# Storing the rows of a seven-product matrix multiply without chained adding transfers, with raw rows, raw weights and gate weights sharing one pool

## The chip, the cores and the metric

The kernel runs on one core of a Trainium2 chip. The metric is the device time of one execution in microseconds (us), the median of the runs. The engines are PE (TensorE, matmul), PEld (its weight loads), DVE (VectorE), ACT (ScalarE), POOL (GpSimd) and SP (SyncE, which here only issues DMAs). POOL issues DMAs too, all those that add to what lies at the destination among them.

## The reference, cut to what matters

One layer of an encoder runs over 1024 prompt tokens and 32 sample tokens, which the kernel treats as T = 1056 columns. After two attention branches it ends in three parts:

```python
# ConvFFN
a, g = split(h @ w_up)                     # 1024 -> 2 x 2816
gc = conv_b + sum(conv_w[i] * gx[:, i:i+T] for i in range(3))
f = (gelu(gc) * a) @ w_down                # 2816 -> 1024
x = x + rms_norm(f, g_post_ffn)
# per-layer embedding
gate = sigmoid(rms_norm(x, g_pre_ple) @ w_ple_gate)
x = x + rms_norm(gate * (pe @ w_ple), g_post_ple)
```

Everything is float32. A matmul operand is split into a high part (rounded to float32r) and a low part (the remainder), and each product takes three matmuls: high by high, high by low, low by high.

## The kernel before

**Layout.** Activations lie with features on the 128 partitions and tokens along the row. `HT` = 528 is half of the tokens, `HC` = 264 a quarter; `one` and `two` are the two halves.

**Up product (L1103 to L1316).** The 22 feature tiles `f` of the gated FFN are made one by one, tiles 0 to 3 plainly and tiles 4 to 21 by a seven-product scheme (`up_strassen`, seven `mul` of 24 matmuls of 264 columns each). Per tile `gx` and `av` (three buffers each) take the two halves of `h @ w_up`, and `activate_steps` (L1058) makes the convolution in `gc` (one buffer), its gelu, and the product with `av`. Signs are put in, so that the seven-product scheme of the *down* product finds its operands in the DRAM tile `d_b[7, 11, 128, 528]`: seven sums of the four quarters of the 2816 x 1056 operand (top tiles f < 11 and bottom tiles f >= 11, halves `one` and `two`). Each tile writes its rows into the slots that contain it, from POOL. A top tile stores `one` to slots 0 to 3 (one transfer with a repeated source), `two` to slot 4, and then adds `two` to slots 1 to 3. A bottom tile stores to slots 5 and 6, adds `two` to slots 2 to 4, and then adds `one` to slot 3. The last transfer of either has to wait for the one before it, since both write the same rows.

From L1311 to L1316 (tiles 2 to 20 and the quarter sums) the order on the engines is set by the framework's planner; before and after, PE, DVE and ACT run in an order written out in the program (`manual_schedule`), while the planner still orders SP and POOL.

**Down product (L1322 to L1700).** 28 units `u`, seven operands `p` by four output row groups `m`. A unit is 11 blocks of 128 by 3 matmuls by 2 column halves, 66 matmuls of 264 columns, in three parts `q` (4, 4 and 3 blocks). `row_load` fetches the rows of `d_b` (tile `uraw`, three buffers), `row_split` makes their high and low parts (`d0` to `d8`); `w_load` fetches the raw weights (`wraw`, two buffers, one unit each), `w_split` makes `whi` and `wlo`. All loads go by SP, one after the other. `uraw`, `wraw` and `d0` to `d5` lie in the pool `up`, which is released after unit 27.

Between the parts stand side jobs. `gate_ahead` (L1363) loads a tile of the last part's weights `w_ple_gate` (`raw`, two buffers), splits it (`t`, three buffers) and stores the parts to `d_gate` from POOL: 8 tiles of two parts each. It comes after every part with q = 0 or 2 from unit 1 on (L1654), two parts in a unit. `last_rows_up` finishes tile 21 in unit 0. `norm_first` makes the first half's RMS norms in units 20 to 27 (`NORM_1`).

**Gate phase (L1701 to L1843).** 32 products of 24 matmuls of 264 columns: 16 for set c = 0 (8 output tiles n by two quarters), 8 for c = 1 and 8 for c = 2. The gate weights return from `d_gate` through POOL (`gate_weights`, L1604): tiles 0 and 1 into `whi` and `wlo` in unit 27, the others, 1024 KB each, into `gw` in the space that `up` leaves. Beside the products, `norm_second` makes the norms of the second half; `NORM_2` says how many of its 34 steps follow each product. Its steps 1, 12 and 28 are totals of squares (`total`), its steps 2, 15 and 29 the matmuls on those totals and the inverse roots (`own_sums`, `inverse`); step 20 completes the operand of c = 1 and step 34 that of c = 2. `LAST` places the same for the final norm: `last_total`, `last_sum`, `last_inverse` and `last_rows` (which multiplies, and adds to the output by a POOL transfer). After the last product the tail makes the final norm of c = 2 and stores it.

Of the kernel before, what the change touches and what calls it, by code (L numbers as in the profile page):

```python
# [17 lines left out]
P = 128  # L18
# [88 lines left out]
          (6, 0, 0): 1, (6, 0, 1): 1, (6, 1, 0): 1, (6, 1, 1): 1, (6, 1, 2): 1, (6, 2, 0): 1, (6, 2, 1): 1, (6, 2, 2): 1}  # L107
NORM_2 = (1, 1, 1, 2, 2, 2, 2, 2, 1, 1, 2, 2, 2, 2, 2, 2, 1, 1, 2, 2, 1)
SQUARES_2 = ((6, 0, 2), (6, 1, 0))
# [3 lines left out]
def emit(tc, a):  # L113
# [944 lines left out]
    def activate_steps(f, gx, av):  # L1058
        gc = tl(fp, [P, GW - 2], tag="gc", bufs=1)
        L = GW - 2  # L1060
        cw = [col(CONV_W + 3 * f + i) for i in range(3)]
        ac.activation(gc, gx[:, 0:L], AF.Identity, scale=cw[0], bias=col(CONV_B + f))
        yield
        ve.scalar_tensor_tensor(gc, gx[:, 1 : L + 1], cw[1], gc, op0=ALU.mult, op1=ALU.add)
        ve.scalar_tensor_tensor(gc, gx[:, 2 : L + 2], cw[2], gc, op0=ALU.mult, op1=ALU.add)
        po.tensor_copy(convo[:, f, 0:2], gx[:, NP : NP + 2])
        po.tensor_copy(convo[:, f, 2:4], gx[:, GW - 2 : GW])
        yield
        ac.activation(gc, gc, AF.Gelu_apprx_tanh)
        yield  # L1070
        top = f < HD
        for o, g, neg in ((slice(0, HT), slice(0, HT), not top), (slice(HT, NP), slice(HT, NP), top), (slice(NP, T), slice(NP + 2, None), top)):
            if neg:
                ve.scalar_tensor_tensor(av[:, o], gc[:, g], -1.0, av[:, o], op0=ALU.mult, op1=ALU.mult)
            else:
                ve.tensor_tensor(av[:, o], gc[:, g], av[:, o], op=ALU.mult)
        k = f % HD

        def to(x, i, j, **kw):
            x = x.unsqueeze(1).to_broadcast([P, j - i, HT]) if j > i + 1 else x.unsqueeze(1)  # L1080
            po.dma_start(d_b[i:j, k].rearrange("q p t -> p q t"), x, **kw)

        if top:
            to(av[:, one], 0, 4)
            to(av[:, two], 4, 5)
            to(av[:, two], 1, 4, accum_op=ALU.add)
        else:
            po.dma_start(d_b[5:7, k].rearrange("q p t -> p q t"), av.rearrange("p (q t) -> p q t", q=2))
            to(av[:, two], 2, 5, accum_op=ALU.add)
            to(av[:, one], 3, 4, accum_op=ALU.add)  # L1090

# [232 lines left out]
    WSRC = (quarter_of(0, 0), d_ws[1], d_ws[2], quarter_of(1, 1), quarter_of(0, 1), d_ws[0], d_ws[3])  # L1324
    NU = 4 * len(RSRC)
    up = pool("up", side="right")
    ub = pool("ub", side="right")
# [11 lines left out]
    def row_load(p, i):  # L1339
        if p < len(RSRC):  # L1340
            n = 2 if i < 5 else 1
            raws[p, i] = tl(up, [P, 2, HT], tag="uraw", bufs=3)[:, :n]
            dma.dma_start(raws[p, i], d_b[RSRC[p], 2 * i : 2 * i + n].rearrange("k p t -> p k t"))
# [19 lines left out]
    def gate_ahead(n):  # L1363
        raw = []

        def load():
            raw.append(tl(wp, [P, KT, P], tag="raw", bufs=2))
            dma.dma_start(raw[0], a["w_ple_gate"][n])

        def part(b):  # L1370
            c = slice(KT // 2 * b, KT // 2 * (b + 1))
            t = tl(tp, [P, 2, HT], F32R, tag="t", bufs=3)[:, :, : KT // 2 * P]
            split_rows(t[:, 0], t[:, 1], raw[0][:, c].rearrange("p k c -> p (k c)"), False)
            po.dma_start(d_gate[n].rearrange("p (x b c) -> p x b c", x=2, b=2)[:, :, b], t)

        return [load] + [lambda b=b: part(b) for b in range(2)]
# [3 lines left out]
    def w_load(u):  # L1380
        if u < NU:
            t = tl(up, [P, HD * P], tag="wraw", bufs=2)
            dma.dma_start(t, WSRC[u // 4][u % 4])
            wraw[u] = t.rearrange("p (k c) -> p k c", c=P)
# [202 lines left out]
    row_load(0, 2)  # L1587
    w_load(1)
    for q in range(3):
# [14 lines left out]
    def gate_weights(n):  # L1604
# [8 lines left out]
        else:  # L1613
            t = tl(gw, [P, 2, KT, P], F32R, tag="gw", bufs=KT - 2)
            po.dma_start(t, src)
            for b in range(0, KT, KT // 2):
                for x in range(2):
                    out[x].append(t[:, x, b : b + KT // 2])
        wgate[n] = out
# [5 lines left out]
    for load, *fs in items:  # L1625
        loads.append((len(ahead) - 4, load))
        ahead += fs
    done = 0
    norm = None
    for u in range(NU):  # L1630
# [3 lines left out]
        for q in range(3):  # L1634
            h, l = wsp.pop((u, q))
            for k in range(KS[q], KS[q + 1]):
                wh, wl = h[:, k - KS[q]], l[:, k - KS[q]]
                xh_, xl_ = [t[:, k % 2] for t in rows[p, k // 2]]
                for j in range(2):
# [3 lines left out]
                    pe.matmul(o, wl, xh_[:, s], start=False, stop=(k == HD - 1 and p in (3, 4, 6)), skip_group_check=True)  # L1643
            if q == 0:
                w_load(u + 2)
            w_split(u + 1, q)
# [4 lines left out]
            if (m, q) == (0, 0):  # L1651
                row_split(p, 5)
                row_load(p + 1, 1)
            if (u, q) > (1, 0) and q != 1 and done < len(ahead):  # L1654
                while loads and loads[0][0] <= done:
# [19 lines left out]
            if u == NU - 1 and q:  # L1675
                gate_weights(q - 1)
            for i in range(NORM_1.get((p, m, q), 0)):
                next(norm, None)
# [27 lines left out]
    norm = norm_second()  # L1706
    gate_weights(2)

# [46 lines left out]
    def gated(n, t, g):  # L1755
        zz = z[:, n, SETS[2]]
        ve.tensor_tensor(zz, t, g, op=ALU.mult)
        if n < KT - 2:
            sq = ag[2] if n == 0 else tl(gw, [P, HC], tag="sq1", bufs=2)
            ac.activation(sq, zz, AF.Square)  # L1760
        else:
            sq = tl(gw, [P, HC], tag="sq1", bufs=2)
            ve.tensor_tensor(sq, zz, zz, op=ALU.mult)
# [5 lines left out]
    def gated_sum():  # L1769
        if len(ends) == 1 and gathered[0] < KT - 3:  # L1770
# [6 lines left out]

    LAST = {(1, 3): [(last_total, 0)], (1, 5): [(last_sum, 0), (last_inverse, 0)], (1, 6): [(last_rows, 0, 0), (last_rows, 0, 2)], (1, 7): [(last_rows, 0, 4), (last_rows, 0, 6)],
            (2, 0): [(last_total, 1)], (2, 2): [(last_sum, 1), (last_inverse, 1)]}
    for i in range(4):  # L1780
        LAST[2, 3 + i] = [(last_rows, 1, 2 * i)]
    gathered = [0]
# [4 lines left out]
    for at, (c, n, j) in enumerate(parts):  # L1787
        s = SETS[c]
        if n == 0 and j == 0:
            ag[c] = tl(np_, [P, 2, HT], tag="acc", bufs=2)[:, 0, : s.stop - s.start]  # L1790
            if c == 2:
                assert next(norm, 0) == 0

                early = tl(gw, [P, 2, HC], tag="early", bufs=1)
                dma.dma_start(early, kpt(d_pl, KT - 2, s))
# [3 lines left out]
        if j == 0:  # L1799
            if c < 2 or n < KT - 2:  # L1800
                tg[c] = tl(gw, [P, HT], tag="plt", bufs=2)[:, : s.stop - s.start]
                dma.dma_start(tg[c], d_pl[n, :, s])
            else:
                tg[c] = early[:, n - KT + 2]
# [10 lines left out]
        after = None  # L1815
        if c == 0 and j == 0 and n + 3 < KT:
            gate_weights(n + 3)
        if at < len(NORM_2):
# [15 lines left out]
    for i in range(3):  # L1834
        if i == 2:
            after()
        pe.matmul(ps, onesM, (ag[2], *ends)[i], start=(i == 0), stop=(i == 2))
    gain(KT - 1)
    rs = tl(np_, [P, HT], tag="rs", bufs=1)[:, :HC]
    inverse(rs, [(ps, slice(0, HC))])  # L1840
# [5 lines left out]
    np_.release()  # L1846
    gw.release()
    wp.release()
    cst.release()
# [84 lines left out]
```

## Time and profile before

| what | value |
|---|---|
| time, median of 3 runs | 2004.07 us (2000.85 to 2005.7) |
| the profiled execution: its own time | 2003.85 us |
| the profiled execution: its span | 2001.9 us |
| mean granted TensorE clock | 0.988 |
| busy in the span: PE, DVE, ACT, POOL | 1938.0, 1234.7, 951.2, 422.7 us |
| up product of tiles 4 to 21 (1258 to 1631.6 us) | DMA share 0.65 in 1258 to 1620 |
| down product | 1631.6 to 1878.7 us |
| gate phase and tail | 1878.7 to 2001.9 us |

PE is counted busy while a matmul runs, at whatever clock; matmuls of 264 columns start some 0.12 us apart at full clock and some 0.22 us apart at half. The window view gives for each stretch the busy time of an engine with the number of its instructions, the granted clock, and the DMA engines' mean share.

### The profile page before, as it was taken

Reading aid. Unit: us, or ns where it says so; the run is one execution under the profiler, and the core shown is the slowest. Engines: PE = TensorE matmul, PEld = TensorE weight load, DVE = VectorE, ACT = ScalarE, POOL = GpSimd, SP = SyncE. Lnnn points to the kernel's source line nnn. Section 1 sums busy time; section 2 is a strip of 40 time slices with the busy share of each in tenths; the row PEclk is TensorE's granted clock in tenths of the full one; section 3 lists DMA queues with packets and bytes.
Section 4 is the critical chain, followed back from the end, with each engine's and each line's share of the span. In section 5 each row is a group of like instructions: output and inputs, shape, how many; then the busy total and the mean of one; then the engine's idle time right before and its main releaser. Section 6 shows DMA issues by size and latency. Waiting matters only on the chain.

```text
span 2001.9 us, 34483 instructions
## 1 busy us (share of the span) xinstructions
PE 1938.0 (97%) x13594; PEld 1895.5 (95%) x13594; DVE 1234.7 (62%) x2524; ACT 951.2 (48%) x1747; POOL 422.7 (21%) x479
## 2 busy tenths in 40 slices
PE   8999999999999999999999999999999998999996
PEld 7999999999999999998999999999999998999996
DVE  7556655466376474665644775776676754558675
ACT  6456456354473553662423454433333344545454
POOL 4423322242121131121220111212122111000102
PEclk9999999999999999998999999999999998999998
DMA  7112111266244272247733447866656579956636
GB/s 282 64 56 84 62 56 59 72 184 164 79 135 110 90 190 72 83 129 233 266 124 114 130 137 243 243 156 165 138 130 134 122 221 310 330 175 222 214 121 109
DMA packets 112382, 300.94 MB, mean 150 GB/s; under 512 B 11796, under 2 KB 34012, under 8 KB 111324
## 3 DMA queue, kind: packets, MB, share of 16 engines
q1 hardware_dynamic: 78780, 198.45, 30.3%
q0 software_dynamic: 33152, 99.94, 20.2%
q8 instruction: 106, 1.74, 0.3%
q14 instruction: 56, 0.46, 0.1%
q10 hardware_dynamic: 288, 0.36, 0.1%
HBM read 198.49 MB, written 123.28 MB: 161 GB/s over the span
## 4 chain that ended last, share of the span: by engine, by line
PE 70%; DVE 13%; DMA 6%; ACT 6%; issue 3%; SPq 0%; POOL 0%; DVEq 0%; ACTq 0%; POOLq 0%
PE mm L228 12%; PE mm L229 12%; PE mm L230 12%; PE two L1208 6%; PE two L1210 6%; PE two L1209 6%; PE two L1643 2%; PE two L1641 2%; PE two L1642 2%; PE one L508 2%; PE two L730 2%; DMA d_b<-av 2%; PE one L466 1%; DVE d L698 1%; DMA ev<-d_inv 1%
## 5 line engine op out<-in xcount | busy, mean ns | idle before, releaser
L228 PE MATMUL mm<-xh,whi 128*128 128x352 f32 x1248 | 412.1, 330 | 0.0
L230 PE MATMUL mm<-xh,wlo 128*128 128x352 f32 x1248 | 411.9, 330 | 0.0
L229 PE MATMUL mm<-xl,whi 128*128 128x352 f32 x1248 | 409.7, 328 | 0.0
L208 POOL TENSOR_TENSOR wlo<-raw,whi 128x512 fp32r<-128x512 f32 x130 | 188.0, 1452 | 678.8 <-ACT whi L207 626.3
L228 PEld LDWEIGHTS mm<-xh,whi 128*128 128x128 f32 x1248 | 235.2, 188 | 1.6 <-DVE ev L352 0.5
L229 PEld LDWEIGHTS mm<-xl,whi 128*128 128x128 f32 x1248 | 235.0, 188 | 1.7 <-issue 0.3
L230 PEld LDWEIGHTS mm<-xh,wlo 128*128 128x128 f32 x1248 | 234.6, 188 | 1.1
L1641 PE MATMUL two<-d,whi 128*128 128x264 f32 x616 | 178.1, 289 | 9.6 <-ACT whi L1391 7.5
L1643 PE MATMUL two<-d,wlo 128*128 128x264 f32 x616 | 177.9, 289 | 1.4 <-DVE wlo L1392 1.3
L1642 PE MATMUL two<-d,whi 128*128 128x264 f32 x616 | 177.9, 289 | 1.0 <-DVE d L1351 0.9
L207 ACT ACTIVATE whi<-raw 128x512 fp32r<-128x512 f32 (+1 forms) x146 | 89.5, 621 | 157.6 <-PE mm L229 95.2
L1210 PE MATMUL two<-mh,wlo 128*128 128x264 f32 x576 | 163.1, 284 | 0.0
L1209 PE MATMUL two<-ml,whi 128*128 128x264 f32 x576 | 163.0, 284 | 0.0
L1208 PE MATMUL two<-mh,whi 128*128 128x264 f32 x576 | 161.2, 284 | 0.0
L1641 PEld LDWEIGHTS two<-d,whi 128*128 128x128 f32 x616 | 118.4, 192 | 10.6 <-ACT whi L1391 8.3
L1643 PEld LDWEIGHTS two<-d,wlo 128*128 128x128 f32 x616 | 118.3, 192 | 2.6 <-DVE wlo L1392 2.6
L1642 PEld LDWEIGHTS two<-d,whi 128*128 128x128 f32 x616 | 118.4, 192 | 1.7 <-DVE d L1351 1.7
L1210 PEld LDWEIGHTS two<-mh,wlo 128*128 128x128 f32 x576 | 108.4, 188 | 0.0
L1209 PEld LDWEIGHTS two<-ml,whi 128*128 128x128 f32 x576 | 108.4, 188 | 0.0
L1208 PEld LDWEIGHTS two<-mh,whi 128*128 128x128 f32 x576 | 107.4, 188 | 0.0
L352 DVE TENSOR_TENSOR ev<-mm,rstd 128x352 f32<-128x352 f32 x120 | 61.4, 518 | 54.4 <-PE mm L230 53.9
L1198 ACT ACTIVATE whi<-ws 128x512 fp32r<-128x512 f32 x72 | 45.5, 633 | 102.1 <-PE two L1209 75.5
(503 smaller groups left out, 5184.1 us busy)
## 6 DMA issues: line engine op xcount, KB each, us to landing
raw<-in_w_in SPq DMA_DIRECT2D x52, 512.0 KB, 3.8
uraw<-d_b SPq DMA_DIRECT2D x36, 528.0 KB, 4.8
d_b<-av POOLq DMA_DIRECT2D x22, 792.0 KB, 9.2
d_ws<-in_w_down POOLq DMA_DIRECT2D x24, 704.0 KB, 11.7
raw<-in_w_up SPq DMA_DIRECT2D x27, 512.0 KB, 4.1
d_b<-av POOLq DMA_DIRECT2D x11, 1056.0 KB, 5.0
wraw<-d_ws SPq DMA_DIRECT2D x16, 704.0 KB, 7.9
sraw<-in_w_up SPq DMA_DIRECT2D x17, 512.0 KB, 4.9
```

The source lines that it names most:

```text
L207: ac.activation(hi[-1][:, d], raw[:, b], AF.Copy)
L208: eng.tensor_tensor(lo[-1][:, d], raw[:, b], hi[-1][:, d], op=ALU.subtract)
L228: pe.matmul(ps, h, xh(kt), start=(first and i == 0), stop=False)
L229: pe.matmul(ps, h, xl(kt), start=False, stop=False)
L230: pe.matmul(ps, l, xh(kt), start=False, stop=(last and i == n - 1))
L352: return lambda ps, s: ve.tensor_tensor(t[:, s], ps, rstd(s), op=ALU.mult)
L1208: pe.matmul(ps[:, j, :HC], w[0][:, k], x[0][:, k, s], start=st, stop=False, skip_group_check=True)
L1209: pe.matmul(ps[:, j, :HC], w[0][:, k], x[1][:, k, s], start=False, stop=False, skip_group_check=True)
L1210: pe.matmul(ps[:, j, :HC], w[1][:, k], x[0][:, k, s], start=False, stop=sp_, skip_group_check=True)
L1641: pe.matmul(o, wh, xh_[:, s], start=(k == 0 and p in (0, 4, 5)), stop=False, skip_group_check=True)
L1642: pe.matmul(o, wh, xl_[:, s], start=False, stop=False, skip_group_check=True)
L1643: pe.matmul(o, wl, xh_[:, s], start=False, stop=(k == HD - 1 and p in (3, 4, 6)), skip_group_check=True)
```

## The change

1. *Rows.* VectorE adds the two halves once (`sm`, written over `gc`). A top tile stores `one` and `two` to slots 0 and 4 in one transfer and `sm` to slots 1 to 3; nothing is added in DRAM. A bottom tile stores to slots 5 and 6, adds `two` to slots 2 and 4, and adds `sm` to slot 3. No transfer of a tile writes rows that another of the same tile writes.
2. *Pool.* `uraw` and `wraw` move to a pool `rp` that lives to the end. Gate weights 2 and 3 go into these buffers and are asked for in unit 27; the others (`gw`, now four buffers) are asked for two tiles earlier. The buffers `plt`, `early` and `sq1` of the gate phase move into tiles that exist already.
3. *Gate splits.* They come one in a unit, after q = 2, from unit 4 to unit 19, and each raw tile is asked for two parts later in the list than before. `w_load(1)` stands after the first part of unit 0.
4. *Steps.* `NORM_2` has a product more between total and sums at three places, and its last step stands after product 22 in place of 20. The entries of `LAST` come two products later; the last two rows of c = 1 are done in the tail.

```diff
-NORM_2 = (1, 1, 1, 2, 2, 2, 2, 2, 1, 1, 2, 2, 2, 2, 2, 2, 1, 1, 2, 2, 1)
+NORM_2 = (1, 0, 1, 2, 2, 2, 2, 2, 2, 0, 1, 2, 2, 2, 2, 2, 2, 1, 0, 1, 2, 2, 1)
...
+        both, sm = av.rearrange("p (q t) -> p q t", q=2), gc[:, :HT]
+        ve.tensor_tensor(sm, av[:, one], av[:, two], op=ALU.add)
         if top:
-            to(av[:, one], 0, 4)
-            to(av[:, two], 4, 5)
-            to(av[:, two], 1, 4, accum_op=ALU.add)
+            to(both, slice(0, 5, 4))
+            to(sm, slice(1, 4))
         else:
-            po.dma_start(d_b[5:7, k].rearrange("q p t -> p q t"), av.rearrange("p (q t) -> p q t", q=2))
-            to(av[:, two], 2, 5, accum_op=ALU.add)
-            to(av[:, one], 3, 4, accum_op=ALU.add)
+            to(both, slice(5, 7))
+            to(av[:, two], slice(2, 5, 2), accum_op=ALU.add)
+            to(sm, slice(3, 4), accum_op=ALU.add)
...
+    rp = pool("rp", side="right")
...
-            raws[p, i] = tl(up, [P, 2, HT], tag="uraw", bufs=3)[:, :n]
+            raws[p, i] = tl(rp, [P, 2, HT], tag="uraw", bufs=3)[:, :n]
...
-            t = tl(up, [P, HD * P], tag="wraw", bufs=2)
+            t = tl(rp, [P, HD * P], tag="wraw", bufs=2)
...
     row_load(0, 2)
-    w_load(1)
     for q in range(3):
...
-            t = tl(gw, [P, 2, KT, P], F32R, tag="gw", bufs=KT - 2)
-            po.dma_start(t, src)
+            if n < 4:
+                t = [tl(rp, [P, HD * P], F32R, tag="wraw", bufs=2) if n == 2 else tl(rp, [P, 2, HT], F32R, tag="uraw", bufs=3).rearrange("p k t -> p (k t)") for x in range(2)]
+                t = [v[:, : KT * P].rearrange("p (k c) -> p k c", c=P) for v in t]
+                for x in range(2):
+                    po.dma_start(t[x], src[:, x])
+            else:
+                t = tl(gw, [P, 2, KT, P], F32R, tag="gw", bufs=KT - 4)
+                po.dma_start(t, src)
+                t = [t[:, x] for x in range(2)]
...
-        loads.append((len(ahead) - 4, load))
+        loads.append((len(ahead) - 2, load))
...
             if q == 0:
+                if u == 0:
+                    w_load(1)
                 w_load(u + 2)
...
-            if (u, q) > (1, 0) and q != 1 and done < len(ahead):
+            if u >= 4 and q == 2 and done < len(ahead):
...
                 gate_weights(q - 1)
+                gate_weights(q + 1)
...
-    gate_weights(2)
+    gate_weights(4)
...
+        sq = g if n else ag[2]
...
-    LAST = {(1, 3): [(last_total, 0)], (1, 5): [(last_sum, 0), (last_inverse, 0)], (1, 6): [(last_rows, 0, 0), (last_rows, 0, 2)], (1, 7): [(last_rows, 0, 4), (last_rows, 0, 6)],
-            (2, 0): [(last_total, 1)], (2, 2): [(last_sum, 1), (last_inverse, 1)]}
-    for i in range(4):
-        LAST[2, 3 + i] = [(last_rows, 1, 2 * i)]
+    LAST = {(1, 5): [(last_total, 0)], (1, 7): [(last_sum, 0), (last_inverse, 0)], (2, 0): [(last_rows, 0, 0), (last_rows, 0, 2)], (2, 1): [(last_rows, 0, 4), (last_rows, 0, 6)],
+            (2, 2): [(last_total, 1)], (2, 4): [(last_sum, 1), (last_inverse, 1)]}
+    for i in range(3):
+        LAST[2, 5 + i] = [(last_rows, 1, 2 * i)]
+    plt, turn = tl(rp, [P, 2, HT], tag="uraw", bufs=3), 0
...
-                early = tl(gw, [P, 2, HC], tag="early", bufs=1)
+                early = tl(np_, [P, 2, HT], tag="accn", bufs=1)[:, :, :HC]
...
-                tg[c] = tl(gw, [P, HT], tag="plt", bufs=2)[:, : s.stop - s.start]
+                tg[c] = plt[:, turn % 2, : s.stop - s.start]
...
-        if c == 0 and j == 0 and n + 3 < KT:
-            gate_weights(n + 3)
+        if c == 0 and j == 0 and n + 5 < KT:
+            gate_weights(n + 5)
...
     gain(KT - 1)
+    last_rows(1, KT - 2)
```

More of the change, by code (lines that the diff above doesn't have):

```diff
@@ L1077, in activate_steps, with to @@
         k = f % HD
-        def to(x, i, j, **kw):
-            x = x.unsqueeze(1).to_broadcast([P, j - i, HT]) if j > i + 1 else x.unsqueeze(1)
-            po.dma_start(d_b[i:j, k].rearrange("q p t -> p q t"), x, **kw)
+        def to(x, q, **kw):
+            o = d_b[q, k].rearrange("q p t -> p q t")
+            po.dma_start(o, x if len(x.shape) == 3 else x.unsqueeze(1).to_broadcast([P, o.shape[1], HT]), **kw)
+        both, sm = av.rearrange("p (q t) -> p q t", q=2), gc[:, :HT]
+        ve.tensor_tensor(sm, av[:, one], av[:, two], op=ALU.add)
         if top:
-            to(av[:, one], 0, 4)
-            to(av[:, two], 4, 5)
-            to(av[:, two], 1, 4, accum_op=ALU.add)
-        else:
-            po.dma_start(d_b[5:7, k].rearrange("q p t -> p q t"), av.rearrange("p (q t) -> p q t", q=2))
-            to(av[:, two], 2, 5, accum_op=ALU.add)
-            to(av[:, one], 3, 4, accum_op=ALU.add)
+            to(both, slice(0, 5, 4))
+            to(sm, slice(1, 4))
+        else:
+            to(both, slice(5, 7))
+            to(av[:, two], slice(2, 5, 2), accum_op=ALU.add)
+            to(sm, slice(3, 4), accum_op=ALU.add)
     def plain_out(gx, av, j, s, ps):
@@ L1371, in part @@
             c = slice(KT // 2 * b, KT // 2 * (b + 1))
-            t = tl(tp, [P, 2, HT], F32R, tag="t", bufs=3)[:, :, : KT // 2 * P]
+            t = tl(tp, [P, 2, KT // 2 * P], F32R, tag="t", bufs=3)
             split_rows(t[:, 0], t[:, 1], raw[0][:, c].rearrange("p k c -> p (k c)"), False)
@@ L1613, in gate_weights @@
         else:
-            t = tl(gw, [P, 2, KT, P], F32R, tag="gw", bufs=KT - 2)
-            po.dma_start(t, src)
+            if n < 4:
[7 more added lines that the diff above has]
+                t = [t[:, x] for x in range(2)]
             for b in range(0, KT, KT // 2):
                 for x in range(2):
-                    out[x].append(t[:, x, b : b + KT // 2])
+                    out[x].append(t[x][:, b : b + KT // 2])
         wgate[n] = out
@@ L1757, in gated @@
         ve.tensor_tensor(zz, t, g, op=ALU.mult)
+        sq = g if n else ag[2]
         if n < KT - 2:
-            sq = ag[2] if n == 0 else tl(gw, [P, HC], tag="sq1", bufs=2)
             ac.activation(sq, zz, AF.Square)
         else:
-            sq = tl(gw, [P, HC], tag="sq1", bufs=2)
             ve.tensor_tensor(sq, zz, zz, op=ALU.mult)
@@ L1800, in emit @@
             if c < 2 or n < KT - 2:
-                tg[c] = tl(gw, [P, HT], tag="plt", bufs=2)[:, : s.stop - s.start]
+                tg[c] = plt[:, turn % 2, : s.stop - s.start]
+                turn += 1
                 dma.dma_start(tg[c], d_pl[n, :, s])
@@ L1847, in emit @@
     gw.release()
+    rp.release()
     wp.release()
```

## The prediction

> **What bounds the kernel now.** I read the page first, then PE's waits from the up product to the end, then a window table of PE over that stretch, then time lines around the losses. Page:
>
> ```profile
> span 2001.9 us, 34483 instructions
> PE 1938.0 (97%) x13594; PEld 1895.5 (95%) x13594; DVE 1234.7 (62%) x2524; ACT 951.2 (48%) x1747; POOL 422.7 (21%) x479
> ```
>
> PE is the bound, and the diff leaves its matmuls as they are. So the change is worth the PE time that is lost where it acts, and the tail. The PE windows (length, PE busy with its count, clock, DMA share, GB/s):
>
> ```profile
> 1270.00:1276.60 6.60, 3.23 (x16) 0.79 0.77 252
> 1276.60:1620.00 343.40, 343.40 (x2819) 1.00 0.63 148
> 1631.60:1642.00 10.40, 7.42 (x39) 0.69 1.06 355
> 1642.00:1673.70 31.70, 31.41 (x253) 0.99 0.86 270
> 1673.70:1686.20 12.50, 5.86 (x26) 0.62 1.04 292
> 1867.00:1878.70 11.70, 9.66 (x69) 1.00 0.45 106
> 1908.00:1915.00 7.00, 5.11 (x30) 0.79 0.56 170
> 1947.00:1950.00 3.00, 2.39 (x18) 1.00 0.02 2
> 1964.00:1970.00 6.00, 4.36 (x22) 0.73 1.12 213
> 1983.50:2001.90 18.40, 2.14 (x6) 0.69 0.60 99
> ```
>
> The second row is the yardstick: 343.40 us by 2819 is 0.1218 us a matmul. Length less count times 0.1218 is what a window lost, idle time and half clock together: (A) 1270: 4.65; (B) 1631: 5.65, and 0.88 in the window after it; (C) 1673: 9.33; (D) 1867: 3.30; (E) 1908: 3.35; (F) 1947: 0.81; (G) 1964: 3.32. Together 31.3 us. The busy column hides part of it: after a gap PE works on, at clock 0.62 to 0.79.
>
> Here stands a rule of the Trainium skill, "TensorE: Matmul & The Clock Gate", section "HAM oscillation — how this bites in real kernels": the clock falls after gaps of more than about 3.4 us. The windows at 1908 and 1964 differ from it: idle 1.9 and 1.6 us there, clock 0.79 and 0.73. By that rule these two would cost their idle time only, and the forecast would come out some 3 us higher; the sum below goes by the rows.
>
> **The change part by part.**
>
> *Row stores, A.* DVE's write of `av` for tile 4 needs the buffer of tile 1, which its adding store still reads:
>
> ```profile
> 1256.12 1.36 POOL L1081 DMA_DIRECT2D d_b<-av  x2 [2.65 <-DVE av L1076]
> 1263.07 1.27 POOL L1081 DMA_DIRECT2D d_b<-av  x1 [5.59 <-DMA d_b<-av]
> 1272.61 0.70 DVE L1261 TENSOR_TENSOR av<-p,two 128x528 f32<-128x528 f32 x1 [3.50 <-DMA d_b<-av]
> ```
>
> POOL waited until 1263.07 for the first stores, and the adding one landed some 9 us later. After the change `av` is read by one plain store of two slots, issued near 1256 and landed by 1263 (the two before, five slots, took until then): 9 us ahead of the need. A goes: -4.6. What is late next is `gc`: one buffer, now read by the store of `sm`, so that the next tile's ACT L1062 must wait for that landing. For a top tile this is about 7 us after the issue (five slots as before); only tiles 2 and 3, whose L1062 followed the multiplication within 1 us, shift by 7 us. ACT is in order, with `whi` behind it, but `whi` has four buffers, three products of 24 x 0.1218 = 2.9 us ahead, 8.8 us of cover. I take +1 us, between 0 and +6 (a whole landing, unhidden). For a bottom tile:
>
> ```profile
> 1436.36 0.76 POOL L1088 DMA_DIRECT2D d_b<-av  x1 [2.78 <-DVE av L1076]
> 1437.16 1.28 POOL L1081 DMA_DIRECT2D d_b<-av  x1
> 1447.60 0.90 POOL L1081 DMA_DIRECT2D d_b<-av  x1 [4.15 <-DMA d_b<-av]
> 1448.94 1.27 ACT L1062 ACTIVATE gc<-gx,vec 128x1058 f32<-128x1058 f32 x1 [0.29 <-DVE gx L1275]
> 1448.14 0.70 DVE L1275 TENSOR_TENSOR gx<-p,two 128x528 f32<-128x528 f32 x1 [0.65 <-PE two L1210]
> ```
>
> Three slots of adding landed in 10.4 us. After the change two slots and one are added, the same 792 KB, with 0.7 us of DVE (an add of 528, last row) and some 0.9 us of issue in front of the second: `gc` is free at 1448.3 to 1449.2, against 1448.94 now. That is inside the cover of 8.8 us: 0. The `sm` add itself, 22 x 0.7 = 15 us of DVE, lies beside a DVE that is 62% busy: 0, and without that cover 0.7 us a tile. For tile 21, inside the written order, +0.3.
>
> For the adding store the Trainium skill, "DMA: Bandwidth & Descriptors", section "Anatomy of one DMA — SWDGE (gpsimd) path", gives 2.0 us plus bytes over 436 GB/s, an estimate of 3.9 us for 792 KB; the row has 10.4 us. By that formula `gc` is never late and the +1 would be 0.
>
> *Down start, B.* PE stops at 1633 for rows (0, 1):
>
> ```profile
> 1623.03 0.33 SPq L1383 DMA_DIRECT2D wraw<-in_w_down  x1
> 1623.45 1.23 SPq L1343 DMA_DIRECT2D uraw<-d_b  x2
> 1624.73 0.51 SPq L1383 DMA_DIRECT2D wraw<-in_w_down  x1
> 1634.19 1.08 ACT L1350 ACTIVATE d<-uraw 128x1056 fp32r<-128x1056 f32 x1 [5.21 <-DMA uraw<-d_b]
> 1622.52 1.31 POOL L1081 DMA_DIRECT2D d_b<-av  x1
> ```
>
> They were issued at 1623.45 and competed with tile 20's adding store, which is the same 792 KB after the change. `w_load(1)`, now later in the program, stood behind these rows anyway; taking it away can only help rows (0, 3) and (0, 4). B stays; -0.5 of the 0.88 behind it. Ends: 0 and -6.5.
>
> *Gate splits, C.* The chain reads upward:
>
> ```profile
> 1656.02 1.31 POOL L1081 DMA_DIRECT2D d_b<-av  x1
> 1670.76 0.88 POOL L1081 DMA_DIRECT2D d_b<-av  x1 [13.42 <-DMA d_b<-av]
> 1671.33 2.51 POOL L1374 DMA_DIRECT2D d_gate<-t  x3
> 1679.41 0.63 ACT L1350 ACTIVATE t<-raw 128x512 fp32r<-128x512 f32 x1 [9.76 <-DMA d_gate<-t]
> 1680.61 0.59 PE L1641 MATMUL two<-d,whi 128*128 128x264 f32 x1 [6.64 <-ACT whi L1391]
> 1669.02 0.63 ACT L1391 ACTIVATE whi<-wraw 128x512 fp32r<-128x512 f32 x1 [5.33 <-DMA wraw<-d_ws]
> ```
>
> POOL stood 13.42 us on tile 21's second adding store, three `d_gate` stores behind it; the fourth gate split found no free `t`, ACT stood 9.76 us, and `whi` for unit 4 behind it, and PE. After the change POOL has no such wait and the first gate split comes after unit 4's last part. Either is enough: -9.3. What is late next is the raw weight load in the last row, which ACT awaited until 1669.02 while PE, at 66 x 0.1218 = 8.0 us a unit, enters unit 4 near 1671; high and low part take 0.6 + 0.7, so 0.6 us are to spare. The gate traffic that shared the DMA (share 0.86) goes, so I leave it at 0; ends 0 and +5. The 16 splits later cost ACT 0.6 and DVE 0.7 each, one in a unit of 8 us: 0, under units that lose nothing now; DVE would bear it as long as a unit leaves 1 us.
>
> *D* lies under `NORM_1`, which is untouched: 0.
>
> *Gate weights and steps, E to G.*
>
> ```profile
> 1880.53 3.18 POOL L1615 DMA_DIRECT2D gw<-d_gate  x6
> 1904.36 0.71 DVE L1498 TENSOR_TENSOR zd<-zd,res 128x528 f32<-128x528 f32 x1 [7.38 <-DMA res<-d_x]
> 1910.21 0.42 ACT L1436 ACTIVATE y<-accn 128x264 fp32r<-128x264 f32 x1 [1.46 <-DVE accn L1433]
> 1949.68 0.70 DVE L1510 TENSOR_TENSOR el<-zd,eh 128x528 fp32r<-128x528 f32 x1
> 1961.66 2.80 DVE L1732 SCALAR_TENSOR_TENSOR zd<-zd,vec,rs 128x528 f32<-128x528 f32 x4
> 1965.29 0.43 DVE L1752 TENSOR_TENSOR acc<-acc,sig 128x264 f32<-128x264 f32 x1 [0.49 <-ACT sig L1748]
> ```
>
> Six loads of 1024 KB fill the DMA after 1880.53, the residual load lies among them, DVE stands 7.38 us and the total for E's sums is late (1910.21). With tiles 2 and 3 brought in unit 27, four loads are left, a third less, and a product more (2.9 us) stands between total and sums. The gap of about 2 us goes, and with it the half clock: -3.3. The two tiles now in unit 27 fall into a window of DMA share 0.45: 0; they precede tile 1's weights on POOL's queue, which could cost up to 2.
>
> F is `last_sum(0)` behind a busy DVE, two products after its total as before: 0 (to -0.8). G is `last_sum(1)`: in front of its total stand eight multiplications of 0.7 (two groups as in L1732) and only then the last addition of the square sum, 1965.29. Both move by two products, so the rows are in front again; but the square sum is complete two products earlier. I take -2.5 of 3.3; ends 0 and -3.3.
>
> The last step of `norm_second` goes from product 20 to 22, by 5.8 us. It ended at 1950.4; c = 2 starts with the 25th product, 1878.7 + 24 x 2.92 plus the 5 us of E, F and sums, near 1954. So it would be 2 us late if DVE lagged as now, and the seven us it no longer waits in E make up for most: +0.5, ends 0 and +3.
>
> *Tail.* Two multiplications of 0.4 us are added; between the squares and the next step DVE waits now:
>
> ```profile
> 1988.11 0.43 DVE L1470 TENSOR_TENSOR y<-y 128x264 f32<-128x264 f32 x1 [1.68 <-ACT y L1469]
> 1990.75 2.42 POOL L1739 DMA_DIRECT2D out_y<-zd  x2 [6.00 <-DVE zd L1734]
> ```
>
> They fit into the 1.68; the added store takes 1.2 us of POOL, inside its 6.00, but shares the DMA with the last stores: +0.8, ends 0 and +3.
>
> **Sum**, on the profiled execution's 2003.85 us (span 2001.9 plus 2 around it, 0.2 below the median of 2004.07): -4.6 + 1 + 0.3 - 0.5 - 9.3 - 3.3 - 2.5 + 0.5 + 0.8 = -17.6, so 1986. All eight losses gone: 1972.6.
>
> **The rivals.**
>
> 1. *The waits move.* Raw weights late at unit 4 (up to +5 with half clock), the `gc` wait unhidden after A (+6), gate tile 1 (+2): 1999. For it: the slack of 0.6 us; against it: DMA traffic falls in each place.
> 2. *The rows still chain*, because the planner takes slots 2 and 4 (or 0 and 4) for a range that holds the slots between. Then `sm` waits for a landing as before, `gc` is free 6 to 10 us later, near the cover; C still goes. About half of A is lost, and 0.3 us at each of 11 tiles: 1992.
> 3. *B goes too*, with D, once SP and POOL are less crowded: 1986 - 5.7 - 3.3 = 1977. For it: DMA share 1.06 there; against: the same stores and rows compete.
> 4. *Slower*: `gc`'s single buffer stops PE in the up product. Place: ACT L1062 of the 11 bottom tiles. The longest landing above is 14.4 us (1656.02 to the end of POOL's wait), 4 us more than at 1437. If that came at every tile and passed to PE, 11 x 4 = 44 us; slower begins where 24 us pass, 2.2 us a tile. At 3 us: 1986 + 33 = 2019. Against it: three products of cover.
>
> **How the numbers follow.** Forecast 0.57, rival 1 0.15, rival 2 0.08, rival 3 0.10, rival 4 0.10. About 0.3%, 6 us, is what a measurement of this kernel can tell from no change. Faster by more (below 1998): forecast, 2, 3 and a third of 1, 0.80; the same: 0.10; slower: 0.10. Range: from 1974, nearly all losses gone, to 2001, past rival 1; left out are rival 4 and the ends. The forecast's own is 1978 to 1994.
>
> **What would show it.** Right: no PE gap near 1270 on L1261; POOL's waits on `d_b` transfers nearly gone; no ACT wait on `d_gate`; DVE's wait on `res` below 3 us; no clock drop at E. Wrong: L1062 waiting for `d_b` transfers with `whi` late behind it; L1391 waiting for `wraw` at units 1 to 5 with PE idle; PE idle at the start of c = 2.

## The result and the profile after

The changed kernel takes 1986.65 us (median of 4 runs, 1985.63 to 1987.79) against 2004.59 (4 runs on the same chip): a ratio of 0.9914, 95% interval 0.9897 to 0.9931. Forecast were 1986 and a range of 1974 to 2001. The profiled execution took 1986.21 us, its span is 1984.5 us, 17.4 less than before. One execution of old_steps, an experiment below, took 6560.14 us against 1981 to 1986 for its other three, and its median and ratio leave it out. The total came out as forecast, but its parts did not: two of them missed by almost 4 us each, in opposite directions.

The page of the kernel after (span; busy time of each engine):

```profile
span 1984.5 us, 34506 instructions
PE 1929.8 (97%) x13594; PEld 1889.1 (95%) x13594; DVE 1251.3 (63%) x2546; ACT 951.5 (48%) x1747; POOL 407.6 (21%) x470
```

DVE has 16.6 us more, of which 22 additions of 0.7 us make 15.4; PE runs the same 13594 matmuls. The window view of PE after the change (length, PE busy with its count, clock, DMA share, GB/s):

```profile
1257.50:1620.00 362.50, 362.50 (x2979) 1.00 0.46 126
1625.60:1640.00 14.40, 8.62 (x51) 0.92 0.84 283
1640.00:1655.00 15.00, 14.29 (x113) 0.96 0.92 298
1655.00:1850.00 195.00, 195.00 (x1610) 1.00 0.83 264
1850.00:1866.00 16.00, 13.22 (x98) 1.00 0.42 103
1866.00:1961.40 95.40, 95.40 (x786) 1.00 0.58 169
1961.40:1984.50 23.10, 3.68 (x8) 0.59 0.64 94
```

Where PE is busy for the whole length of a window and the clock is 1.00, nothing is lost: rows 1, 4 and 6. So the stops A (1270), C (1673), E, F and G (1908 to 1966) are all gone. What is left stands in three places: the start of the down product (rows 2 and 3), the norm at 1850 to 1866 (D, row 5), and a tail that is longer than before (row 7). PE's waits from 1225 us to the end (in total, times, longest) name them:

```profile
PE one L1850 <- DVE acc L1787: 5.1, 1, 5.1
PE two L1650 <- ACT whi L1394: 2.9, 2, 1.5
PE two L1651 <- DVE d L1354: 2.9, 2, 2.0
PE two L1652 <- DVE wlo L1395: 2.0, 4, 0.9
PE two L1650 <- ACT d L1353: 1.3, 1, 1.3
```

The first line is the tail. The third and fifth stand at the start of the down product. The second and fourth stand partly there and partly at D: 1.5 us of the second and 1.1 us of the fourth end at 1855 to 1861. A ledger by stretches shows where the span went. It is cut at the first matmul of the up product's scheme, the starts of the first and last of the down product, and the end of the last of the gate products:

| stretch | before | after | difference | forecast |
|---|---|---|---|---|
| to the up product's first matmul | 1258.1 | 1257.5 | -0.6 | 0 |
| from there to the down product's first | 373.5 | 369.8 | -3.7 | -3.6 (A, `gc`) |
| down product | 247.3 | 238.9 | -8.4 | -9.5 (B, C, `sm` of tile 21) |
| gate phase | 104.4 | 95.3 | -9.1 | -5.3 (E, G, end of `norm_second`) |
| tail | 18.6 | 23.0 | +4.4 | +0.8 |
| span | 2001.9 | 1984.5 | -17.4 | -17.6 |

**Tile 1's stores and tile 4.** POOL's and then ACT's and DVE's time lines after:

```profile
1255.18 0.72 POOL L1081 DMA_DIRECT2D d_b<-av  x1 [3.34 <-DVE av L1074]
1256.85 0.77 POOL L1081 DMA_DIRECT2D d_b<-gc  x1 [0.95 <-ACT whi L1199]
1262.76 1.27 ACT L1062 ACTIVATE gc<-gx,vec 128x1058 f32<-128x1058 f32 x1 [0.54 <-DMA d_b<-gc]
1279.17 1.27 ACT L1062 ACTIVATE gc<-gx,vec 128x1058 f32<-128x1058 f32 x1 [3.36 <-DMA d_b<-gc]
1263.56 0.70 DVE L1262 TENSOR_TENSOR av<-p,two 128x528 f32<-128x528 f32 x1 [0.59 <-PE two L1211]
```

DVE's write of `av` for tile 4 now waits for PE (0.59 us), no longer for a transfer (3.50 us before). The price is in the third and fourth rows: the next tiles' L1062 wait for the store of `gc`, 3.36 us at the longest. Over the whole kernel ACT waits so for 12.2 us at 7 tiles:

```profile
ACT gc L1062 <- DMA d_b<-gc: 12.2, 7, 3.4
```

All 7 come before 1363 us, at top tiles. None of it reaches PE, as the first window shows.

**The start of the down product.** SP's row for the first rows before, then its time line, its wait there, and ACT's first steps, after:

```profile
1613.59 0.38 SPq L1343 DMA_DIRECT2D uraw<-d_b  x1
...
1617.09 0.38 SPq L1346 DMA_DIRECT2D uraw<-d_b  x1
1617.52 0.47 SPq L1386 DMA_DIRECT2D wraw<-in_w_down  x1
1618.09 1.39 SPq L1346 DMA_DIRECT2D uraw<-d_b  x2
...
SPq L1346 <- PE two L1211: 9.5, 1, 9.5
...
1626.64 0.63 ACT L1394 ACTIVATE whi<-wraw 128x512 fp32r<-128x512 f32 x1 [4.14 <-DMA wraw<-in_w_down]
1629.64 1.08 ACT L1353 ACTIVATE d<-uraw 128x1056 fp32r<-128x1056 f32 x1 [2.37 <-DMA uraw<-d_b]
```

The first rows leave at 1617.09, 10 us ahead of the down product's first matmul (1627.3), in one burst with everything else; before, they left at 1613.59, 18 us ahead of it (1631.6). The load has waited 9.5 us for a matmul whose result it doesn't read.

**The tail.** DVE's wait before, then DVE's and PE's time lines after:

```profile
1971.42 0.43 DVE L1757 TENSOR_TENSOR zd<-plt,sig 128x264 f32<-128x264 f32 x1 [4.43 <-DMA plt<-d_pl]
...
1957.92 0.43 DVE L1769 TENSOR_TENSOR zd<-uraw,sig 128x264 f32<-128x264 f32 x1 [3.92 <-DMA uraw<-d_pl]
1966.16 0.43 DVE L1787 TENSOR_TENSOR acc<-acc,sig 128x264 f32<-128x264 f32 x1
1966.64 1.25 PE L1850 MATMUL one<-acc,onesM 128*128 128x264 f32 x2 [5.11 <-DVE acc L1787]
```

DVE waits 3.92 us for a row of the per-layer embedding, the fourth of c = 2. Before, it waited as long (4.43 us), but for the second row and 12 us before the last gate matmul, so that it caught up. Now the wait ends 3.5 us before that matmul, the inverse root of c = 1 (L1476, at 1962.49) follows, and the sum that PE needs is complete 5 us after PE's last product.

### The profile page after: what moved, and what is told of

Read it like the earlier page. It is cut to its first block, busy times and chain, and to the rows that moved or that the text cites. A ratio compares the mean times of both kernels' runs of the same rounds, so it can differ in the third digit from the quotient of the medians.

```text
span 1984.5 us, 34506 instructions
## 1 busy us (share of the span) xinstructions
PE 1929.8 (97%) x13594; PEld 1889.1 (95%) x13594; DVE 1251.3 (63%) x2546; ACT 951.5 (48%) x1747; POOL 407.6 (21%) x470
## 4 chain that ended last, share of the span: by engine, by line
PE 77%; DVE 12%; ACT 5%; DMA 4%; issue 3%; SPq 0%; POOL 0%; DVEq 0%; ACTq 0%
PE mm L228 13%; PE mm L229 13%; PE mm L230 13%; PE two L1209 6%; PE two L1211 6%; PE two L1210 6%; PE two L1652 2%; PE two L1651 2%; PE two L1650 2%; PE one L508 2%; PE two L730 2%; PE one L466 1%; DVE d L698 1%; DMA ev<-d_inv 1%; DMA uraw<-d_b 1%
## 5 line engine op out<-in xcount | busy, mean ns | idle before, releaser
L1650 PE MATMUL two<-d,whi 128*128 128x264 f32 x616 | 176.0, 286 | 4.2 <-ACT whi L1394 2.9
L1651 PE MATMUL two<-d,whi 128*128 128x264 f32 x616 | 175.7, 285 | 2.9 <-DVE d L1354 2.9
```

What stands on the lines that cost most here:

```text
L1650: pe.matmul(o, wh, xh_[:, s], start=(k == 0 and p in (0, 4, 5)), stop=False, skip_group_check=True)
L1651: pe.matmul(o, wh, xl_[:, s], start=False, stop=False, skip_group_check=True)
```

## The experiments

Each was timed beside the kernel before, on the same chip; ratios are to that. The last four columns cut the span of the one profiled execution as above (from the up product's first matmul), in us. That execution need not be a median one: for rows_only it is the slowest of five, 4 us above the median, for splits_only and norm2_only the fastest, 3 and 4 us below it.

| kernel | median us | ratio (95%) | to down | down | gate | tail |
|---|---|---|---|---|---|---|
| before | | | 373.5 | 247.3 | 104.4 | 18.6 |
| after | 1986.65 | 0.9914 (0.9897 to 0.9931) | 369.8 | 238.9 | 95.3 | 23.0 |
| rows_only | 1992.76 | 0.9938 (0.9924 to 0.9951) | 368.3 | 244.7 | 103.4 | 20.0 |
| splits_only | 1997.29 | 0.9966 (0.9953 to 0.9978) | 374.4 | 238.7 | 102.5 | 20.4 |
| old_last | 1988.97 | 0.9919 (0.9907 to 0.9932) | 370.3 | 240.2 | 100.9 | 20.2 |
| rows_ahead | 1984.52 | 0.9900 (0.9886 to 0.9913) | 369.3 | 240.6 | 95.3 | 19.3 |
| row_early | 1993.12 | 0.9938 (0.9923 to 0.9952) | 378.1 | 238.7 | 95.3 | 22.8 |
| rows_undone | 1994.99 | 0.9945 (0.9930 to 0.9959) | 378.8 | 238.6 | 95.5 | 23.5 |
| both_ahead | 1990.36 | 0.9924 (0.9908 to 0.9940) | 378.2 | 236.9 | 95.3 | 19.1 |
| old_norm2 | 1984.87 | 0.9895 (0.9880 to 0.9910) | 369.6 | 239.5 | 95.1 | 21.0 |
| ahead_norm2 | 1980.96 | 0.9877 (0.9863 to 0.9890) | 370.3 | 238.7 | 95.3 | 16.9 |
| old_steps | 1981.69 | 0.9885 (0.9870 to 0.9901) | 370.1 | 239.8 | 96.9 | 16.4 |
| norm2_only | 2005.74 | 1.0001 (0.9991 to 1.0010) | 373.5 | 246.0 | 102.9 | 20.9 |
| gc_held | 2051.28 | 1.0236 (1.0218 to 1.0254) | 399.1 | 269.1 | 95.5 | 23.6 |

The kernel before took 2004.31 us in the session of rows_only to rows_ahead, 2006.83 in that of row_early to old_norm2, 2005.02 in that of the last four.

### Which part ends A and C

**rows_only** is the kernel before with the new row stores and nothing else.

```diff
-            to(av[:, two], 4, 5)
-            to(av[:, two], 1, 4, accum_op=ALU.add)
+            to(both, slice(0, 5, 4))
+            to(sm, slice(1, 4))
```

> The kernel before with the new row stores alone (old pool, old gate splits, old steps). My theory: the stop on av near 1270 goes (up product 5 us shorter), and the stop of 6.6 us at unit 4 goes too, since POOL no longer stands 13 us on a d_b transfer with d_gate stores behind it: together 13 to 15 us less than before, 1990; the totals at 1908 and 1964 still stop PE. Rival: the gate splits have to be later as well for unit 4: only 5 us less, 1999.

PE's longest waits in it from 1255 us on:

```profile
PE two L1644 <- DVE wlo L1393: 4.4, 7, 1.6
PE one L1456 <- ACT y L1437: 4.3, 3, 2.5
```

No stop at L1261 is left (to the down product 368.3 us, 5.2 less), and the 6.64 us at unit 4 shrink to waits of 1.7 us at most, for `whi` and `wlo`. But the down product takes only 2.6 us less than before: between 1660 and 1720 us, by 0.1218 us a matmul, 4.7 us are still lost in short stops. ACT waits there for the raw weights, 14.1 us in four times, which is the path of rival 1. E and G stay (second line, 4.3 us, with F).

**splits_only** is the kernel before with the later gate splits and loads.

```diff
-        loads.append((len(ahead) - 4, load))
+        loads.append((len(ahead) - 2, load))
-            if (u, q) > (1, 0) and q != 1 and done < len(ahead):
+            if u >= 4 and q == 2 and done < len(ahead):
```

> The kernel before with the later gate splits alone (one in a unit from unit 4 on, raw tiles asked for two parts later). My theory: unit 4's stop goes (9 us), the one near 1270 stays: 1995. Rival: POOL's wait on tile 21's adding store is only passed on to another stop, since the first gate splits then meet the raw weight load: 2000 or more.

```profile
PE two L1208 <- DVE av L1261: 3.3, 1, 3.3
```

The longest of PE's waits: A is there (3.3 us). Unit 4 no longer appears among them; E and G do (3.2 us for `y`). The down product takes 238.7 us in place of 247.3. So C falls by the gate splits alone, and A by the stores alone. Of C the stores alone end the long stop and, in this profiled execution, about half of the loss. As that is the slowest of its five, a median one may keep less: by the medians rows_only gains 11.6 us, and A and C as forecast, 13.9, less the 2.3 us that the next section finds given back, would be as much. "Either is enough" was right of the splits; of the stores it is likely and not shown.

**rows_undone** takes the other road: the changed kernel with the old row stores (the diff of rows_only, reversed).

> The changed kernel with the old row stores (chained adding transfers). My theory: the stop on av near 1270 is back (5 us), unit 4's is not, since the gate splits come later: 1992. Rival: the chain also holds the down start or unit 4: 1995 or more.

```profile
PE two L1208 <- DVE av L1261: 5.4, 1, 5.4
```

PE's longest wait: A comes back (5.4 us), C doesn't. The ratio is 0.9945 against 0.9914 for the changed kernel, so in it the new stores are worth some 0.3%, about A; the two intervals (0.9930 to 0.9959 and 0.9897 to 0.9931) just touch.

### What the new stores cost later

The runs answer a question that they weren't made for: why the start of the down product got worse. The window view of PE over it, for before, splits_only and rows_undone (old stores), then rows_only and after (new stores):

```profile
1626.00:1662.00 36.00, 32.72 (x239) 0.91 0.96 308
```

```profile
1626.00:1660.00 34.00, 29.66 (x220) 0.95 0.96 310
```

```profile
1629.00:1662.00 33.00, 28.56 (x203) 0.90 0.96 308
```

```profile
1620.00:1660.00 40.00, 33.14 (x253) 0.96 0.90 275
```

```profile
1620.00:1655.00 35.00, 28.51 (x208) 0.95 0.91 291
```

Length less 0.1218 us a matmul is the loss: 6.9, 7.2 and 8.3 us with the old stores, 9.2 and 9.7 with the new. The other kernels below that keep order there fall in with this: 7.1 for norm2_only, 9.7 to 10.9 for old_last, rows_ahead, old_norm2, ahead_norm2 and old_steps. So 2.8 us of what A gave are given back here between before and after, and most of them come with the stores: in the two pairs that differ by the stores alone, the loss is 2.3 us larger with the new ones in the kernel before (9.2 against 6.9) and 1.4 in the changed one (9.7 against 8.3). The rest of the change adds some 1 us (8.3 against 6.9 to 7.2); of it the new pool was not run alone. How the stores do it stays open. Tile 20 writes 528 KB plainly and 792 KB by adding just ahead of the burst in either form, and the same distance before PE's last up matmul. The new form has three transfers there in place of two, and the old one's third came only at 1635.19.

**row_early** was to test whether the first rows come late: they were given a buffer of their own, the tile that later is `d5`.

```diff
-            raws[p, i] = tl(rp, [P, 2, HT], tag="uraw", bufs=3)[:, :n]
+            raws[p, i] = tl(up, [P, 4 * HT], tag="d5", bufs=1)[:, : 2 * HT].rearrange("p (k t) -> p k t", k=2) if (p, i) == (0, 0) else tl(rp, [P, 2, HT], tag="uraw", bufs=3)[:, :n]
```

> The changed kernel with the first raw rows of the down product read into the tile d5, at the base of the pool up, where uraw lay before the change. My theory: in the pool rp these rows lie over an operand of the up product, so that their load waits for PE until 1617 (before: 1613.6) and pushes the first weights and the next rows back; with it the loss at the down start (9.4 us between 1625.6 and 1655 in the changed kernel, 6.5 before) falls by 2 to 3 us: 1984. Rival: the loss comes from tile 20's adding stores alone: no change, 1986 to 1987.

SP's time line and ACT's in it:

```profile
1615.88 2.37 SPq L1346 DMA_DIRECT2D uraw<-d_b  x3
...
1618.92 0.56 SPq L1346 DMA_DIRECT2D d<-d_b  x1
...
1632.32 1.08 ACT L1353 ACTIVATE d<-d 128x1056 fp32r<-128x1056 f32 x1 [16.14 <-DMA d<-d_b]
```

It went the other way. The load of the first rows (`d<-d_b`) was not issued earlier but last of the burst, where the planner, which orders SP, put it. ACT stood 16.14 us for it and PE 9.7 us. So this run leaves the question that was meant open. The trace of rows_only, with the old pool, answers most of it: there the first rows leave at 1608.80, 18 us ahead of the first matmul as before, and the loss is 9.2 us all the same, so late first rows are not what makes it. What row_early does show is that the order inside this burst of 4 us is worth 8 us in the profiled execution (378.1 to the down product against 369.8), and some 5 us by the ratios.

**both_ahead** joins it with rows_ahead (below).

> The changed kernel with the embedding rows of c = 2 fetched four ahead and the first raw rows in d5. My theory: both gains add, 2 us each: 1982. Rival: the row's gain is lost in the units after it: 1984.5 as with the rows fetched ahead alone.

It has the same stop of 9.8 us, and the tail of rows_ahead (19.1 us): the two edits do not touch each other.

### What ends E, F and G

**old_norm2** is the changed kernel with the old `NORM_2`.

```diff
-NORM_2 = (1, 0, 1, 2, 2, 2, 2, 2, 2, 0, 1, 2, 2, 2, 2, 2, 2, 1, 0, 1, 2, 2, 1)
+NORM_2 = (1, 1, 1, 2, 2, 2, 2, 2, 1, 1, 2, 2, 2, 2, 2, 2, 1, 1, 2, 2, 1)
```

> The changed kernel with the old NORM_2 (no product more between total and sums, last step after product 20). My theory: gate tiles 2 and 3 in unit 27 alone take away DVE's wait of 7 us on the residual load, so that most of the loss at E (3.35 us) stays away; at most a gap of 1 us without half clock: 1987 to 1988. Rival: the step between total and sums is what counts: PE stops 2 us and runs at half clock again, 1990.

The gate phase takes 95.1 us, as with the new list, with no stop at E. The tail is shorter (21.0).

**norm2_only** is the other half: the kernel before with the new `NORM_2` (the diff reversed).

> The kernel before with the new NORM_2 alone. My theory: DVE still loses 7 us on the residual load (the six gate tiles still fill the DMA), the product more in front of the sums hides 2.9 us of that, so that PE's stop at E is gone or below 0.5 us, but step 34, two products later, now stops PE at the start of c = 2 by 2 us: 2003 to 2005, no change. Rival: the added product is what ends E without a price: 2000 or less.

PE's waits in it, from the gate phase on:

```profile
PE mm L229 <- DVE el L1510: 4.5, 1, 4.5
...
PE one L1455 <- ACT y L1436: 0.6, 1, 0.6
```

E's stop is gone here too (0.6 us in place of 3.6 for the three sums) although DVE still waits 5.6 us for the residual, but PE then waits 4.5 us for the operand of c = 2, whose last step was moved back. The ratio is 1.0001: the wait was moved, not removed. This is the stop that the forecast feared for the changed kernel (+0.5, up to +3). In the changed kernel DVE waits for the residual nowhere, and the stop isn't there.

**old_last** is the changed kernel with the old `LAST` and all of `last_rows` beside the products.

```diff
-    LAST = {(1, 5): [(last_total, 0)], (1, 7): [(last_sum, 0), (last_inverse, 0)], ...
+    LAST = {(1, 3): [(last_total, 0)], (1, 5): [(last_sum, 0), (last_inverse, 0)], ...
-    last_rows(1, KT - 2)
```

> The changed kernel with the final norm's steps (LAST) where they were before, two products earlier, and the last two rows back in the loop. My theory: the tail, 23.1 us from the last product's end in the changed kernel against 18.6 before, goes back to about 19, since the late load of the third gate row then has three products to be made up; but the sums after product (2, 2) stop PE again by 2 us and half clock (3.3 us): 1985 to 1986. Rival: the sums were late before only because DVE had lost 7 us on the residual load, so they do not stop PE now: 1982.

```profile
PE mm L229 <- DVE el L1513: 2.7, 1, 2.7
...
PE one L1458 <- ACT y L1439: 0.5, 1, 0.5
```

G's own wait stays small (last line, 0.5 us), but this alone doesn't show what ended it, since PE now stops before it (first line); old_steps does. The old places set DVE's rows beside the last steps of `norm_second`, and the operand of c = 2 comes 2.7 us late; the gate phase takes 100.9 us. Half of that loss returns in the tail (20.2).

**old_steps** goes the whole way: old `NORM_2`, old `LAST`, and the rows fetched four ahead as in rows_ahead. Of the change, the stores, the pool and the splits are left.

> The changed kernel with all steps where they were before (old NORM_2, old LAST, the last two rows in the loop), and the embedding rows of c = 2 fetched four ahead. My theory: the early gate tiles alone end the losses E and G, since DVE no longer loses 7 us on the residual load; the gate phase stays at 95 to 97 us and the tail at 18.6 to 19: 0.987 to 0.988 of the time before. Rival: without the products in between, the totals are late again at E and G and PE falls to half clock twice: gate phase 101 us, 0.991.

```profile
PE one L1458 <- ACT y L1439: 1.1, 1, 1.1
```

The gate phase takes 96.9 us, of 104.4 before, with every step in its old place. The stores and the splits alone leave E and G (4.3 and 3.2 us above). DVE's wait for the residual, which made E late, goes the same way: 7.4 us before, 8.1 in rows_only, 7.0 in splits_only, but 2.1 in old_norm2, 0.9 here and none in the changed kernel. So the pool, with the gate weights that come earlier, ended them. That is by exclusion: the pool was not run alone, nor were the stores and splits together. The new places are worth 1.6 us of gate phase at most, and cost 0.5 in the tail against ahead_norm2 (16.4 against 16.9).

### What lengthened the tail, and a better version

**rows_ahead** is the changed kernel with the embedding rows of c = 2 (264 columns) fetched four ahead, in quarters of the same buffer, in place of two ahead in halves.

```diff
-                tg[c] = plt[:, turn % 2, : s.stop - s.start]
+                tg[c] = plt[:, turn % 2, : s.stop - s.start] if c < 2 else plt[:, n // 2 % 2, n % 2 * HC : (n % 2 + 1) * HC]
```

> The changed kernel with the embedding rows of c = 2 fetched four ahead in quarters of the same buffer in place of two ahead. My theory: DVE's wait of 3.9 us on the third row (its load issued just behind four adding output stores) goes, the inverse of c = 1 comes some 4 us earlier, and the tail shrinks from 23.1 to 19 to 20 us: 1983. Rival: the load is late because the DMA queues are full of the adding stores, and a buffer that is free earlier changes nothing: 1986 to 1987.

```profile
PE one L1850 <- DVE acc L1787: 1.6, 1, 1.6
```

DVE's wait for the rows is gone, PE's wait in the tail falls from 5.1 to 1.6 us, the tail from 23.0 to 19.3. The gate phase is unchanged. So most of the tail's growth was this one late row. Some of the rest can come without the new steps: with the old ones the tail takes 18.6 us before, but 20.0 in rows_only and 20.4 in splits_only.

**ahead_norm2** adds the old `NORM_2` to it.

> The changed kernel with the embedding rows of c = 2 fetched four ahead and the old NORM_2. My theory: both act on the same thing, the DVE work that is left for the last products, so their gains (0.9900 and 0.9895 of the time before, against 0.9914 for the changed kernel) add only in part: tail 19 us, gate phase 95 us, 0.988 of the time before, 1981 on a chip with 2004 before. Rival: they add nothing: 0.990.

PE's window in it over the tail:

```profile
1962.20:1979.10 16.90, 2.04 (x6) 0.64 0.86 128
```

The rest of the wait goes as well. The likely reason is that with the new list the later steps of `norm_second` are DVE work that pushes the sums of c = 2 back; the run shows the effect, 2.4 us of tail, and not the way. The tail is shorter than before the change, and the ratio, 0.9877 (0.9863 to 0.9890), is the best of all kernels here. Against old_steps, in the same session, the intervals overlap; which of the two is faster is not settled.

### How deep the cover of `gc` is

**gc_held** is the changed kernel with two more stores of `sm` in each tile, 792 KB each, into a place that nothing reads. They hold the single `gc` buffer longer.

```diff
+        for i in range(2):
+            po.dma_start(d_held[f, 3 * i : 3 * i + 3].rearrange("q p t -> p q t"), sm.unsqueeze(1).to_broadcast([P, 3, HT]))
```

> The changed kernel with two more stores of sm per tile into a DRAM scratch tile that nothing reads (3 slots, 792 KB each), so that gc stays taken longer. My theory (ACT's order has three products of cover): gc is free some 6 us later in each tile, ACT's L1062 waits several us in most of the tiles, and PE loses at most 1 us in the up product before its last tile; the added DMA traffic costs 0 to 4 us at the down start: 1987 to 1992. Rival (gc's single buffer stops PE): 2 us and more in each of 17 tiles, 2020 or more.

My theory fell: the run is 2.4% slower than the kernel before. Two of ACT's waits in it, two of PE's in the up product, a row of ACT's time line in the down product, and PE's longest wait there:

```profile
ACT gc L1063 <- DMA d_held<-gc: 59.7, 15, 14.5
ACT av L1271 <- DMA d_b<-av: 29.8, 11, 4.6
...
PE two L1212 <- ACT av L1271: 7.3, 4, 2.9
PE two L1212 <- DVE av L1265: 5.9, 4, 2.7
...
1705.35 1.27 ACT L1063 ACTIVATE gc<-gx,vec 128x1058 f32<-128x1058 f32 x1 [14.46 <-DMA d_held<-gc]
...
PE two L1653 <- ACT whi L1397: 35.7, 3, 28.3
```

The place that rival 4 named is the up product. There ACT waits for `gc` 31.5 us at 13 tiles, 5.6 us at the longest, and PE waits for `whi` nowhere. Of PE's 19.0 us in 12 stops, 13.2 are the third and fourth lines, for `av`, whose buffers wait for transfers (second line) that POOL issues behind the dummy stores of the tile before. So the way over `whi` stays covered at 5.6 us too, and what PE loses there points to the traffic more than to `gc`.

The long stop is in unit 1 of the down product. ACT stands 14.46 us at L1063 for `gc` (fifth line), after 13.71 for the tile before it; `whi` of the down product is queued right behind (1706.53), and PE waits 28.3 us for it. The three products of cover are the up product's and do not stand between these two. So the path from `gc` over ACT and `whi` to PE exists, in another place than rival 4 put it, and holding and traffic are not told apart by this run.

## Why the prediction was right, and where its parts were not

The total agrees within 1 us by luck: misses of opposite sign cancel.

- **A and `gc`.** A went as forecast. The +1 for `gc` was not there: L1062 does wait, at 7 top tiles in place of the two named (12.2 us), within the cover. But 2 to 3 us come back at the start of the down product. PE's first stop there, 1.4 us, lies in this row of the ledger, so that -3.7 against -3.6 is a coincidence too.
- **B** is the step that failed in kind: "can only help" and "the same 792 KB" left out that the new stores could change the burst. In place of -0.5 the stretch lost 2.8 more (6.9 to 9.7). Its bound of 0 excluded a loss without a row that did so. The rows of the new pool, which SP may load only when PE has read what lay there (9.5 us), were not foreseen either; by rows_undone that is the smaller part.
- **C.** -9.3 as forecast. The splits alone do it (splits_only); that the stores alone do it too is shown of the long stop only (rows_only). The raw weights with their 0.6 us to spare are not late at unit 4, and rival 1 did not come in the changed kernel. In rows_only, where the splits stay early, they are late.
- **D** stayed, at 4.1 us (16.00 less 98 x 0.1218) in place of 3.3; why it grew is open.
- **E to G.** Size too small, -9.1 against -5.3, and the mechanism right in part. F and G were left with 0.8 each and the end of `norm_second` with +0.5; all three are zero. These make 2.1 of the 3.8 missing; the rest is not assigned. And the reason for E was shared between the tiles and the product more between total and sums; old_norm2 shows that the tiles suffice, norm2_only that the steps alone give nothing. For G the forecast counted on the new places in `LAST`; old_steps has them as before, and PE waits 1.1 us there, so most of G went without them.
- **Tail.** The term mis-sized most: +4.4 against +0.8, outside its range of 0 to +3. I priced the two rows and the store that were added to it and did not follow the wait for the embedding rows, which now falls on the fourth row of c = 2, where no product is left to catch up. rows_ahead shows it: 19.3 us with these rows fetched earlier. For A and C the prediction asks what is late next; for the tail it doesn't.
- **Rival 2** fell: no `d_b` transfer of POOL waits for another in the changed kernel. **Rival 3** fell: B grew. **Rival 4** did not happen in the changed kernel, nor in gc_held at the place that it named; gc_held shows the path in the down product.

## What to carry to other kernels

When waits are taken out ahead of a fixed end, follow the next wait of the same engine to that end: a late row that cost nothing 12 us before the last product cost 3.7 us (the tail of the changed kernel against that of rows_ahead) when its wait ended 3.5 us before it. Where two edits each end the same stop, run each alone: here the written steps were credited with what the earlier transfers did, and the best version undoes part of the steps. A burst of loads just before a phase begins deserves a look of its own: here its order was worth 8 us in one profiled execution (row_early), and the form of the stores just ahead of it 1.4 to 2.3 us.

## What was not expected of the hardware

Idle time at the down product's start cost different clocks. From 1620 to 1655 us PE is idle 5.8 us in ahead_norm2 (35.00 less 29.20) and 6.5 in the kernel after, but the granted clock is 0.90 in the first and 0.95 in the second:

```profile
1620.00:1655.00 35.00, 29.20 (x206) 0.90 0.89 286
```

Idle time and clock together are nearly equal all the same (9.9 and 9.7 us). So what a stretch loses can't be read from its idle time alone. The Trainium skill, "TensorE: Matmul & The Clock Gate", section "HAM oscillation — how this bites in real kernels", has the clock fall after gaps of more than about 3.4 us; in these two stretches it falls with no gap above 2.0 us.

A plain store of 792 KB that repeats its source took 5.4 us from issue to landing (the median of 11 on the page of the kernel after), against 9.2 us for the adding ones of the same size (22 on the page before):

```profile
d_b<-av POOLq DMA_DIRECT2D x22, 792.0 KB, 9.2
...
d_b<-gc POOLq DMA_DIRECT2D x11, 792.0 KB, 5.4
```

The formula of the Trainium skill that the prediction weighed ("DMA: Bandwidth & Descriptors", section "Anatomy of one DMA — SWDGE (gpsimd) path") gives an estimate of 3.9 us; both are longer.
